# Where a kernel's one-hot tiles begin in SBUF: moving them by 64 bytes, with every instruction left in its place

## The chip, the cores and the metric

The kernel runs on one core of a Trainium2 chip, as one program. The metric is the device time of one execution in microseconds; lower is better. The time before is 1871.04 us, the median of three runs (1870.9 to 1872.39).

## What is computed

The reference is a small decoder of two layers over 256 tokens of 1024 features, in float32. Each layer is a mixer (sparse and block attention in layer 0, latent attention in layer 1) and then a PEER channel mixer, which takes most of the time and is the only part that the change touches:

```python
q = (xc @ w_q).reshape(t, 8, 2, 128)                    # 8 heads, two halves
sc = einsum('thpc,hpnc->thpn', q, sub_keys)             # 128 keys a half
...                                                     # top 16 of each half, top 16 of their sums
g = softmax(top_s)                                      # 16 gates a head: 128 of 16384 experts a token
u = u_tab[expert]
act = gelu(einsum('thkd,td->thk', u, xc))
w = g * act
return einsum('thk,thkd->td', w, v_tab[expert])
```

The kernel does not gather experts. It computes all 16384 activations of every token, multiplies them by a dense matrix of gates (zero for experts that were not chosen), and multiplies the result by the whole `v_tab`.

## The kernel before, in words

**Exact products from split operands.** A float32 product is made of three passes in the format fp32r: both operands are split into a high part and a low rest (`hi`, `lo`), and high by high, high by rest and rest by high are added up in PSUM. Weights arrive by DMA in tiles `raw` of 128x1024, in three buffers. `Weights.split` (L69 on ScalarE, L70 on VectorE) turns each half of such a tile into a 128x512 `hi` and `lo`, five buffers of each.

**The PEER block, once a layer (`peer`).** Its stretches follow each other on TensorE:

1. Queries: 16 products S of `w_q` with the tokens (`rhi`, `rlo`: 8 chunks of 128x256 each, not normalised), and scores of each query (L1052) against the sub-keys. VectorE takes the top 16 (`stage1`).
2. Blocks: the loop `for b in range(NK)` over 128 blocks of 128 experts. A block is 24 matmuls (L823 to L825): a 128x128 piece of a weight tile is loaded as the stationary operand, and the 256 tokens (`hi`, `lo`, normalised) stream through as the moving operand. The result S goes into the block of `A` by `put_act`.
3. Gates, worked in between the blocks as a background job (`gates`, pumped by `bg.pump(PB)` after each half block): for four tokens at a time, one-hots over the first key (`E`, a tile `ohB`, bf16) and one-hots times gate (`G`, a tile `ohA`, fp16) are made by VectorE (L986 to L1001) and, for every second group, partly by ScalarE (L980, L982). Eight matmuls of 128 columns (L1015, into `scp`) then make the dense gates of the four tokens: `E` is the stationary operand and `G` the moving one. There are 64 such groups a layer, and each stands between two of the matmuls of step 2.
4. Output: `wsplit(b)` splits block b of `A` into a high and a low part (L1092, L1093), into tiles with the names `ohA` and `ohB` too. They are the stationary operand of 12 matmuls of 512 columns a block (L1103 to L1105), with the split rows of `v_tab` as the moving operand; the sum over all blocks stays in four PSUM banks `acc`.

**Where tiles lie.** A pool's tiles lie one behind the other in each partition's bytes. A tile without use (`fill...`) only pushes what comes after it. So the start addresses of the tiles, taken modulo 512 bytes (the residue below), are:

| tiles | role on TensorE | residue before | residue after |
|---|---|---|---|
| `hi`, `lo` of the weights, `raw`, `A[0]` | stationary in blocks, moving in the output | 160 | 160 |
| `rhi`, `rlo`, `hi0`.., `lo0`.. (tokens) | moving in queries and blocks | 96 | 96 |
| `ohB`, `ohA` as one-hots `E`, `G` | stationary and moving of the gates | 160 | 96 |
| `ohA`, `ohB` as split activations | stationary in the output | 160 | 160 |
| `act` (queries, and a helper tile of `put_act`) | stationary in the scores | 160 | 96 |
| `A[1]` (blocks 104 to 127) | none | 160 | 96 |

Within these tiles every operand that TensorE reads starts at a multiple of 512 bytes from the tile's start (or, for the split activations after the change, from 64 bytes into it), so one residue holds for all operands of a row. The second token of a pair in `E` and `G` lies 2 bytes further.

Of the kernel before, what the change touches and what calls it, by code (L numbers as in the profile page):

```python
# [9 lines left out]
F32 = mybir.dt.float32  # L10
F32R = mybir.dt.float32r
# [135 lines left out]
def body(tc, I, out):  # L147
    nc = tc.nc
    with ExitStack() as ctx:
# [24 lines left out]
        for k, v in PLAN1:  # L174
            if k == "P" and v[0] == "c":
                add(I["w1"][int(v[1])], 352)
            elif k == "P":
                n = "uq" if v[0] == "q" else "ukv"
# [102 lines left out]
        def tiles8(pool, name, dtype=F32R):  # L281
            return [pool.tile([128, S], dtype, name=f"{name}{c}") for c in range(8)]
# [475 lines left out]
        def peer(layer, gcol, final=False):  # L758
            with ExitStack() as c1:
# [6 lines left out]
                def scr(n):  # L766
                    o = off[0]
                    off[0] += n
                    assert off[0] <= (NA - SCR) * S, off
                    return flat[:, o:o + n]  # L770

                hp = c1.enter_context(tc.tile_pool(name="hp", bufs=1))
                ohp = c1.enter_context(tc.tile_pool(name="ohp", bufs=2))
# [3 lines left out]
                RE, RM = hp.tile([128, S], BF, name="RE"), hp.tile([128, 2, S], F16, name="RM")  # L777
                RA = hp.tile([128, 3, 4 * len(GA)], F32, name="RA")

                hp.tile([128, 112], F32, name="fill0")  # L780
                hi, lo = tiles8(hp, "hi"), tiles8(hp, "lo")
                hp.tile([128, 16], F32, name="fill1")
                rawc = ExitStack()
                rawpool = rawc.enter_context(tc.tile_pool(name="rawt", bufs=1))
                rawpool.tile([128, 112], F32, name="fill2")
                scv = scr(2 * 16 * 128)
                sc = scv.rearrange("p (a b c) -> p a b c", a=2, b=16)
                sk = scr(2048).rearrange("p (j n) -> p j n", j=16)
# [176 lines left out]
                def gates():  # L965
                    def hot(t0, E, G):
                        pr = lambda r: r.rearrange("p (q t) -> p q t", t=2)[:, :, None, :]
                        bc = lambda r: pr(r[:, t0:t0 + 4]).to_broadcast([128, 2, 128, 2])
                        io = lambda n: iotaX[:, None].to_broadcast([128, n, 128, 2])
                        act = t0 // 4 in GA  # L970
                        e = E[:, 1]
                        if act:
                            k = 4 * GA.index(t0 // 4)

                        def pair(i, relu):
                            if act:
                                for j in (i, i + 1):
                                    r = [RA[:, n, k + j:k + j + 1] for n in range(3)]
                                    if relu:
                                        nc.scalar.activation(e[:, j // 2, :, j % 2], e[:, j // 2, :, j % 2], AF.Relu, bias=r[1], scale=r[2])  # L980
                                    else:
                                        nc.scalar.activation(e[:, j // 2, :, j % 2], iota, AF.Square, bias=r[0], scale=-1.0)  # L982

                        pair(0, False)
                        if act:
                            nc.vector.tensor_tensor(E[:, 0], io(2), pr(R1[:, t0 // 4, 0]).to_broadcast([128, 2, 128, 2]),  # L986
                                                    op=OP.is_equal)
                        else:
                            nc.vector.tensor_tensor(E.rearrange("p s q i t -> p (s q) i t"), io(4),
                                                    pr(R1[:, t0 // 4].rearrange("p s t -> p (s t)")).to_broadcast([128, 4, 128, 2]),  # L990
                                                    op=OP.is_equal)
                        yield YA if act else 0.6
                        pair(2, False)
                        nc.vector.tensor_tensor(G[:, 0], E[:, 0], bc(RM[:, 0]), op=OP.mult)
                        yield YA if act else 0.34
                        pair(0, True)
                        nc.vector.tensor_tensor(G[:, 1], E[:, 0], bc(RM[:, 1]), op=OP.mult)
                        yield YA if act else 0.34
                        pair(2, True)
                        if not act:  # L1000
                            nc.vector.tensor_tensor(e, e, bc(RE), op=OP.mult)  # L1001
                        yield YA if act else 0.34

                    def tiles():
                        return [ohp.tile([128, 4, 128], F32, name=n).rearrange("p t i -> p (t i)").bitcast(d).rearrange(
                            "p (s q i t) -> p s q i t", s=2, q=2, t=2) for n, d in (("ohB", BF), ("ohA", F16))]

                    nxt = tiles()
                    yield from hot(0, *nxt)
                    for t0 in range(0, S, 4):  # L1010
                        E, G = nxt
                        p = ps2.tile([128, 512], F32, name="scp").rearrange("p (t i) -> p t i", t=4)
                        for i in range(4):
                            for s in range(2):
                                nc.tensor.matmul(p[:, i], E[:, 1, i // 2, :, i % 2], G[:, s, i // 2, :, i % 2], start=i + s == 0, stop=True,  # L1015
                                                 skip_group_check=True)
                        if t0 + 4 < S:
                            nxt = tiles()
                            yield from hot(t0 + 4, *nxt)
                        for k, (c, e) in enumerate(((0, NA), (NA, NK))):  # L1020
                            n = min(max(done[0], c), e)
                            if n < e:
                                nc.scalar.activation(A[k][:, n - c:, t0:t0 + 4],
                                                     p[:, :, n:e].rearrange("p t i -> p i t"), AF.Copy)
                            if n > c:
                                a = A[k][:, :n - c, t0:t0 + 4]
                                nc.vector.tensor_tensor(a, a, p[:, :, c:n].rearrange("p t i -> p i t"), op=OP.mult)
                        done[1] = t0 + 4
                        yield 0.5

                def block(b):
                    return A[0][:, b] if b < NA else A[1][:, b - NA]
# [28 lines left out]
                for j in range(16):  # L1061
                    p = ps2.tile([128, 512], F32, name="S")[:, :S]
# [17 lines left out]
                for b in range(NK):  # L1080
                    p = ps2.tile([128, 512], F32, name="S")[:, :S]
# [6 lines left out]
                bg.drain()  # L1088

                def wsplit(b):  # L1090
                    t = ohp.tile([128, 4, 128], F32, name="ohA" if b % 2 else "ohB").rearrange("p (s h) e -> p s (h e)", s=2).bitcast(F32R)
                    nc.scalar.activation(t[:, 0], block(b), AF.Copy)  # L1092
                    nc.vector.tensor_tensor(t[:, 1], block(b), t[:, 0].bitcast(F32), op=OP.subtract)  # L1093
                    return t

                ws = [wsplit(0), wsplit(1)]
                put_act(*prev)
                acc = [[ps2.tile([128, 512], F32, name="acc", bufs=4) for _ in range(2)] for _ in range(2)]
# [8 lines left out]
                for b in range(NK - 2):  # L1107
                    a = ws.pop(0)
                    for dh in range(2):
                        w = W.next()  # L1110
                        if dh == 0:
                            ws.append(wsplit(b + 2))
                        for tb in range(2):
                            mm(b, a, w, tb, dh)
# [5 lines left out]

        even_mixer(0)
        peer(0, 16)
        mla_mixer(8)
        peer(1, 24, True)


# [59 lines left out]
```

## Time and profile before

| what | value |
|---|---|
| time, median of three runs | 1871.04 us (1870.9 to 1872.39) |
| the profiled execution: its time, its span | 1871.02 us, 1869.2 us |
| TensorE busy with matmuls | 1845.6 us, 99% of the span |
| VectorE, ScalarE, GpSimd busy | 1431.8, 1245.3, 15.0 us |
| mean granted clock of TensorE | 0.998 of full speed |
| matmuls L823, L824, L825 on `hi`, `lo` (blocks) | 2048 each |
| matmuls L1015 (gates) | 1024 |
| matmuls L1103 to L1105 (output) | 3072 |

The span is the time from the first to the last instruction; 1.8 us of the profiled time lie outside it. A matmul's busy time in the profile runs from its start to the arrival of its last result, so those of neighbours overlap, and the rate of a stream of matmuls is read from the distance of their starts.

### The profile page before, as it was taken

What the parts mean: (1) busy time and instruction counts of PE and PEld (TensorE: products, weight loads), DVE (VectorE), ACT (ScalarE), POOL (GpSimd) and SP (SyncE); (2) the same over time, 40 slices, a digit from 0 to 9 for tenths busy, and PEclk for the clock granted to TensorE, in tenths of its full rate; (3) what the DMA queues carried; (4) which work ended last, traced back from release to release, by engine and by line L of the source; (5) the groups of instructions that cost most, each with busy time, mean ns of one, the idle gap of its engine ahead of it and who ended that gap; (6) DMA issues with size and microseconds to landing.
All of it is one profiled execution on the core that took longest, in us unless ns stands there. A gap on an engine that the chain in (4) does not pass through costs nothing.

```text
span 1869.2 us, 35589 instructions
## 1 busy us (share of the span) xinstructions
PE 1845.6 (99%) x12568; PEld 1668.6 (89%) x12568; DVE 1431.8 (77%) x3586; ACT 1245.3 (67%) x3060; POOL 15.0 (1%) x34
## 2 busy tenths in 40 slices
PE   9999999999999999999999999999999999999998
PEld 7779999999999888888888899999999988888886
DVE  7968998878897666666677699987888976666665
ACT  5656567888886555555577665688888765555554
POOL 0000000000000000000000000000000000000000
PEclk9999999999999999999999999999999999999999
DMA  6434555555555556565553345655545555555554
GB/s 197 130 112 147 177 188 180 170 168 161 167 161 180 192 193 195 193 195 193 183 170 124 125 148 186 194 170 164 166 161 169 167 183 192 193 193 196 195 192 148
DMA packets 90178, 323.33 MB, mean 173 GB/s; under 512 B 10512, under 2 KB 10896, under 8 KB 89744
## 3 DMA queue, kind: packets, MB, share of 16 engines
q1 hardware_dynamic: 88416, 318.18, 52.9%
q8 instruction: 99, 1.62, 0.4%
q0 software_dynamic: 288, 2.10, 0.3%
q10 hardware_dynamic: 1296, 0.78, 0.1%
q14 instruction: 79, 0.65, 0.1%
HBM read 319.97 MB, written 1.05 MB: 172 GB/s over the span
## 4 chain that ended last, share of the span: by engine, by line
PE 93%; DVE 4%; ACT 1%; issue 1%; DMA 0%; POOL 0%; DVEq 0%; POOLq 0%; ACTq 0%
PE S L823 14%; PE S L825 14%; PE S L824 14%; PE acc L1103 12%; PE acc L1104 12%; PE acc L1105 12%; PE scp L1015 3%; PE pj L301 2%; PE pj L303 2%; PE pj L302 2%; DVE lo L70 1%; PE bk L375 1%; PE scp L1052 1%; PE pj L439 1%; PE pj L440 1%
## 5 line engine op out<-in xcount | busy, mean ns | idle before, releaser
L69 ACT ACTIVATE hi<-raw 128x512 fp32r<-128x512 f32 (+2 forms) x1214 | 755.3, 628 | 562.7 <-DVE lo L70 190.4
L70 DVE TENSOR_TENSOR lo<-raw,hi 128x512 fp32r<-128x512 f32 (+2 forms) x1214 | 825.1, 684 | 361.7 <-ACT hi L69 354.0
L823 PE MATMUL S<-hi,hi 128*128 128x256 f32 x2048 | 584.9, 286 | 0.6 <-ACT A L1044 0.6
L825 PE MATMUL S<-hi,lo 128*128 128x256 f32 x2048 | 575.4, 281 | 0.5
L824 PE MATMUL S<-lo,hi 128*128 128x256 f32 x2048 | 574.4, 281 | 0.0
L825 PEld LDWEIGHTS S<-hi,lo 128*128 128x128 f32 x2048 | 387.2, 189 | 1.7 <-DVE lo L70 1.7
L824 PEld LDWEIGHTS S<-lo,hi 128*128 128x128 f32 x2048 | 388.6, 190 | 0.0
L823 PEld LDWEIGHTS S<-hi,hi 128*128 128x128 f32 x2048 | 385.1, 188 | 1.1 <-ACT A L1044 1.0
L1104 PE MATMUL acc<-lo,ohB 128*128 128x512 f32 x512 | 199.2, 389 | 0.0
L1104 PE MATMUL acc<-lo,ohA 128*128 128x512 f32 x512 | 199.2, 389 | 0.0
L1105 PE MATMUL acc<-hi,ohA 128*128 128x512 f32 x512 | 198.8, 389 | 0.0
L1105 PE MATMUL acc<-hi,ohB 128*128 128x512 f32 x512 | 198.2, 389 | 0.0
L1103 PE MATMUL acc<-hi,ohB 128*128 128x512 f32 x512 | 158.3, 389 | 0.0
L1103 PE MATMUL acc<-hi,ohA 128*128 128x512 f32 x512 | 158.0, 389 | 0.0
L980 ACT ACTIVATE ohB<-ohB,RA 128x128 bf16<-128x128 bf16 x256 | 117.4, 527 | 0.0
L1105 PEld LDWEIGHTS acc<-hi,ohB 128*128 128x128 f32 x512 | 96.2, 188 | 20.0
L1104 PEld LDWEIGHTS acc<-lo,ohA 128*128 128x128 f32 x512 | 96.2, 188 | 19.9
L1103 PEld LDWEIGHTS acc<-hi,ohB 128*128 128x128 f32 x512 | 96.1, 188 | 19.9
L1103 PEld LDWEIGHTS acc<-hi,ohA 128*128 128x128 f32 x512 | 96.1, 188 | 20.0
L1105 PEld LDWEIGHTS acc<-hi,ohA 128*128 128x128 f32 x512 | 96.0, 188 | 19.9
L1104 PEld LDWEIGHTS acc<-lo,ohB 128*128 128x128 f32 x512 | 96.1, 188 | 19.8
L982 ACT ACTIVATE ohB<-iota,RA 128x128 bf16<-128x128 f32 x256 | 84.2, 436 | 0.0
(261 smaller groups left out, 2409.3 us busy)
## 6 DMA issues: line engine op xcount, KB each, us to landing
raw<-in_pu SPq DMA_DIRECT2D x256, 512.0 KB, 3.6
raw<-in_pv SPq DMA_DIRECT2D x256, 512.0 KB, 4.3
raw<-in_pq SPq DMA_DIRECT2D x32, 512.0 KB, 3.6
raw<-in_w SPq DMA_DIRECT2D x20, 512.0 KB, 3.8
raw<-in_uq SPq DMA_DIRECT2D x9, 512.0 KB, 4.3
raw<-in_w SPq DMA_DIRECT2D x12, 352.0 KB, 3.0
raw<-in_w0o SPq DMA_DIRECT2D x8, 512.0 KB, 3.5
raw<-in_w1o SPq DMA_DIRECT2D x8, 512.0 KB, 3.6
```

Of the source, the lines that this page charges most:

```text
L69: self.nc.scalar.activation(hi[:, :w], src, AF.Copy)
L70: self.nc.vector.tensor_tensor(lo[:, :w], src, hi[:, :w].bitcast(F32), op=OP.subtract)
L301: nc.tensor.matmul(ps[tb], hi[c][:, t], a, start=st, stop=False)
L823: nc.tensor.matmul(p, a, hi[c], start=first and i == 0, stop=False)
L824: nc.tensor.matmul(p, a, lo[c], start=False, stop=False)
L825: nc.tensor.matmul(p, b, hi[c], start=False, stop=last and i == 3)
L980: nc.scalar.activation(e[:, j // 2, :, j % 2], e[:, j // 2, :, j % 2], AF.Relu, bias=r[1], scale=r[2])
L982: nc.scalar.activation(e[:, j // 2, :, j % 2], iota, AF.Square, bias=r[0], scale=-1.0)
L1015: nc.tensor.matmul(p[:, i], E[:, 1, i // 2, :, i % 2], G[:, s, i // 2, :, i % 2], start=i + s == 0, stop=True, skip_group_check=True)
L1103: nc.tensor.matmul(o, a[:, 0, t], w[0], start=b == 0, stop=False)
L1104: nc.tensor.matmul(o, a[:, 0, t], w[1], start=False, stop=False)
L1105: nc.tensor.matmul(o, a[:, 1, t], w[0], start=False, stop=b == NK - 1)
```

## The change

The change takes out two filling tiles and enlarges the one-hot tiles from 512 to 640 float32 words. The one-hots use the first 512 words of a tile. The split activations use the words from 16 to 528, which are 64 bytes further on. Without `fill1` the pool `ohp` begins at the tokens' residue; its tiles (2 x 1024 and 4 x 2560 bytes) are a multiple of 512 bytes together, so the pool behind it keeps the tokens' residue without `fill2`.

```diff
                 hp.tile([128, 112], F32, name="fill0")
                 hi, lo = tiles8(hp, "hi"), tiles8(hp, "lo")
-                hp.tile([128, 16], F32, name="fill1")
                 rawc = ExitStack()
                 rawpool = rawc.enter_context(tc.tile_pool(name="rawt", bufs=1))
-                rawpool.tile([128, 112], F32, name="fill2")
...
                     def tiles():
-                        return [ohp.tile([128, 4, 128], F32, name=n).rearrange("p t i -> p (t i)").bitcast(d).rearrange(
+                        return [ohp.tile([128, 640], F32, name=n)[:, :512].bitcast(d).rearrange(
                             "p (s q i t) -> p s q i t", s=2, q=2, t=2) for n, d in (("ohB", BF), ("ohA", F16))]
...
                 def wsplit(b):
-                    t = ohp.tile([128, 4, 128], F32, name="ohA" if b % 2 else "ohB").rearrange("p (s h) e -> p s (h e)", s=2).bitcast(F32R)
+                    t = ohp.tile([128, 640], F32, name="ohA" if b % 2 else "ohB")[:, 16:528].rearrange("p (s e) -> p s e", s=2).bitcast(F32R)
```

No instruction is added, taken out or moved: on each engine and on each DMA queue the instructions of the two programs stand in the same order, with the same shapes and the same engines waited for. They differ in addresses alone (and in line numbers, which are smaller by one behind the edit).

## Rows read from the trace of the kernel before

**Rows 1.** The page's busy times, and its chain that ended last.

```profile
PE 1845.6 (99%) x12568; PEld 1668.6 (89%) x12568; DVE 1431.8 (77%) x3586; ACT 1245.3 (67%) x3060; POOL 15.0 (1%) x34
PE 93%; DVE 4%; ACT 1%; issue 1%; DMA 0%; POOL 0%; DVEq 0%; POOLq 0%; ACTq 0%
```

**Rows 2.** Gate stretches: start:end, length, busy us (count) of PE, PEld, DVE, ACT, POOL.

```profile
306.00:585.00 279.00, 279.00 (x2601) 276.17 (x2599) 236.83 (x557) 231.77 (x709) 0.00 (x0) 1.00 0.52 165
...
1230.00:1509.00 279.00, 279.00 (x2600) 276.17 (x2599) 236.72 (x557) 231.78 (x708) 0.00 (x0) 1.00 0.52 165
```

**Rows 3.** Timeline of TensorE from 216 us: first and last of 104 matmuls (start, us).

```profile
215.76 0.28 PE L825 MATMUL S<-hi,lo 128*128 128x256 f32 x1
...
227.89 0.28 PE L823 MATMUL S<-hi,hi 128*128 128x256 f32 x1
```

**Rows 4.** The same from 276 us: first and last of 109 matmuls.

```profile
275.74 0.28 PE L823 MATMUL S<-hi,hi 128*128 128x256 f32 x1
...
287.98 0.28 PE L823 MATMUL S<-hi,hi 128*128 128x256 f32 x1
```

**Rows 5.** L824 from 216 to 246 us, then from 276 to 288 us (busy, mean ns).

```profile
L824 PE MATMUL S<-lo,hi 128*128 128x256 f32 x85 | 23.8, 281 | 0.0
...
L824 PE MATMUL S<-lo,hi 128*128 128x256 f32 x36 | 9.9, 276 | 0.0
```

**Rows 6.** TensorE's groups from 308 to 584 us, then one from 1230 to 1508 us.

```profile
L824 PE MATMUL S<-lo,hi 128*128 128x256 f32 x690 | 193.9, 281 | 0.0
L825 PE MATMUL S<-hi,lo 128*128 128x256 f32 x689 | 193.8, 281 | 0.0
L1015 PE MATMUL scp<-ohA,ohB 128*128 128x128 f16 x498 | 39.9, 220 | 0.0
...
L824 PE MATMUL S<-lo,hi 128*128 128x256 f32 x695 | 195.3, 281 | 0.0
```

**Rows 7.** Timeline around two groups of gates of layer 0; then around one of layer 1.

```profile
323.37 0.63 PE L1015 MATMUL scp<-ohA,ohB 128*128 128x128 f16 x8
...
324.48 0.28 PE L825 MATMUL S<-hi,lo 128*128 128x256 f32 x1
...
325.16 0.28 PE L825 MATMUL S<-hi,lo 128*128 128x256 f32 x1
325.28 0.63 PE L1015 MATMUL scp<-ohA,ohB 128*128 128x128 f16 x8
...
325.92 0.28 PE L824 MATMUL S<-lo,hi 128*128 128x256 f32 x1
...
326.74 0.28 PE L825 MATMUL S<-hi,lo 128*128 128x256 f32 x1
...
1247.25 0.63 PE L1015 MATMUL scp<-ohA,ohB 128*128 128x128 f16 x8
...
1248.37 0.28 PE L825 MATMUL S<-hi,lo 128*128 128x256 f32 x1
...
1248.71 0.28 PE L825 MATMUL S<-hi,lo 128*128 128x256 f32 x1
```

**Rows 8.** Timeline behind two groups of scores in layer 1's query stretch.

```profile
1068.00 0.28 PE L824 MATMUL S<-rlo,hi 128*128 128x256 f32 x1
...
1069.70 0.28 PE L824 MATMUL S<-rlo,hi 128*128 128x256 f32 x1
1069.93 0.60 PE L1052 MATMUL scp<-A,act 128*128 128x128 f32 x4
...
1070.56 0.28 PE L824 MATMUL S<-rlo,hi 128*128 128x256 f32 x1
...
1071.27 0.28 PE L824 MATMUL S<-rlo,hi 128*128 128x256 f32 x1
```

**Rows 9.** Groups of the output stretch from 600 to 900 us.

```profile
L1104 PE MATMUL acc<-lo,ohA 128*128 128x512 f32 x220 | 85.6, 389 | 0.0
L1105 PE MATMUL acc<-hi,ohA 128*128 128x512 f32 x220 | 85.6, 389 | 0.0
```

## The prediction

> **What bounds the kernel now.** I read the page first. TensorE's matmuls cover 99% of the span, and 93% of the chain that ended last is TensorE's [rows 1]. So what counts is how densely TensorE's matmuls follow each other; the other engines count only where TensorE waits for them. The change touches the block stretch with its gates (one a layer), so I asked for the busy time there. In both stretches TensorE is covered without a hole at the full granted clock, while VectorE works 237 of 279 us and ScalarE 232 [rows 2]. TensorE has to be made faster there, or nothing is.
>
> The timeline shows at what rate it works, and here is something that a share of busy time hides. The same matmul, L823 to L825, runs in two rhythms. From 215.76 to 227.89 us there are 103 distances of starts in 12.13 us: 117.8 ns each [rows 3]. From 275.74 to 287.98 us there are 108 in 12.24 us: 113.3 ns [rows 4]. Shapes, operands and residues are the same in both. The groups show it too: a matmul lasts 281 ns in the slow rhythm and 276 in the fast one [rows 5]. In both gate stretches the means of L824 and L825 are 281 [rows 6], so at least nine in ten of those matmuls are in the slow rhythm.
>
> A rhythm lasts until something interrupts the stream, and the first matmuls behind the interruption set the next one. In the gate stretches the interruptions are the 64 groups of gates a layer. The group at 323.37 us is followed by the fast rhythm (324.48 to 325.16 us: 6 distances in 0.68 us, 113 ns), the group at 325.28 us by the slow one (325.92 to 326.74 us: 7 in 0.82 us, 117 ns) [rows 7]. The same group of layer 1, at 1247.25 us, is followed by the fast one again (3 in 0.34 us) [rows 7]. So the choice is not noise: it repeats at the same place of the program. Behind other interruptions both rhythms occur: between two groups of scores the stream is fast (1068.00 to 1069.70 us: 15 distances, 113 ns), behind the second of these groups slow (1070.56 to 1071.27 us: 6, 118 ns) [rows 8].
>
> **The change part by part.**
>
> *Instructions.* None is added, removed or moved, and no wait changes. The filling tiles cost no instruction; the larger tiles cost memory alone. This is 0 us.
>
> *Work of VectorE and ScalarE on one-hots, `act` and `A[1]`, now 64 bytes lower.* No row has one of these instructions at both residues. Their cover is VectorE's 42 us and ScalarE's 47 us of idle time in each gate stretch [rows 2]: all their work there would have to grow by 18 to 20% before TensorE waited. Likewise faster writes would give nothing. I take 0.
>
> *Output stretch.* The split activations keep residue 160, but half of the new tiles begin 512 bytes off their old place modulo 1024. The stationary operand takes such steps already: L1104 reads the high part, L1105 the low part 1024 bytes behind it, each at two places 512 bytes apart, and both last 389 ns [rows 9]. I take 0. If the steady rate were lost, each of the 3072 matmuls is two streams of 256 columns long, and the difference of the two rhythms, 4.5 ns a stream, would make 3072 x 9 ns = 28 us. I give that no more than 3 in 100 and leave it out of the range.
>
> *The gates' own matmuls.* Stationary `E` and moving `G` lay at 160 and both lie at 96 now, so inside a group of eight nothing changes in relation to each other: 0. For bounds, a step as large as that between the rhythms, 4.5 ns, on each of the 1024 of them is 4.6 us either way.
>
> *The hand-overs.* This is where the change can act. The first weights behind a group (residue 160) are loaded while the last `G` streams: both at 160 before, 160 against 96 now. The latter is the relation that weights and tokens have all through the blocks. And the first `E` is loaded while tokens stream: 160 against 96 before, both at 96 now. If weight loads and moving reads disturb each other by address, the hand-overs shift by some nanoseconds, and a hand-over decides between 113.3 and 117.8 ns for all that follows up to the next group. From 308 to 584 us there are 690 of L824, so some 2,070 matmuls of L823 to L825, and 2,085 in the other stretch [rows 6]: 4,155 together. At nine tenths in the slow rhythm, 3,740 x 4.5 ns = 16.8 us is all that can be won. Falling either way by halves, as behind other interruptions, would win 0.4 x 4,155 x 4.5 ns = 7.5 us. Losing the last tenth costs 0.1 x 4,155 x 4.5 ns = 1.9 us.
>
> Which end? The present order of residues sends nearly every hand-over the slow way, which is an extreme; new relations can hardly make it more so. I take the middle of the two upper ends, 12 us.
>
> The Trainium skill speaks against any effect. Its page "TensorE: Matmul & The Clock Gate" (section "Step-by-step: what each phase is for") has two independent read ports, one for the moving operand and one for weight loads, so that loading the next weights takes nothing from the running matmul. Its section "Back-to-back issue gap" gives columns / 2.4 + 2.5 ns, an estimate of 109.2 ns for 256 columns. By the first rule addresses could not matter and the sum would be 0; the trace has neither rhythm at the second's figure, so something does hold these pairs of load and matmul back. No run here shows yet whether it is an address.
>
> **Sum.** 0 + 0 + 0 + 0 - 12 us, from the profiled execution's 1871.02 us (span 1869.2 and 1.8 outside), which is the median of the runs to 0.02 us: 1859 us.
>
> **The rivals.**
>
> *A. The hand-overs turn (my forecast).* For it: the choice is made within nanoseconds, is the same at the same place in both layers, and the change alters just what TensorE reads at that moment. Own range 1853 to 1865 us: 16.8 us and something from the gates' matmuls at one end, 7.5 us less 1.5 for other stretches at the other.
>
> *B. Nothing turns.* TensorE's two reads may not meet by address, or the shift leaves the hand-overs on the slow side, as they are now. For it: a rhythm changes without any change of address [rows 3, 4], so timing alone decides, and no row shows a residue at work. Against it: a choice this one-sided [rows 6] has a fixed cause, and the operands at the hand-over are the nearest one. Time 1871.0, by 1.9 us for the last tenth of the slow rhythm, and as much the other way: 1869 to 1873 us. By the skill's rule of two ports this is the outcome.
>
> *C. The gates' loads collide (slower).* `E` is now loaded against tokens, and `G` streams against loads, at other relations than before. If each gate matmul loses the step between the rhythms, and the rest of the fast rhythm goes too, 1024 x 4.5 ns + 1.9 us = 6.5 us: 1877.5 us. It decides from 3.7 us on, which is 3.6 ns on each gate matmul or 29 ns on each of the 128 hand-overs. Against it: the pair `E`, `G` keeps its relation.
>
> **How the numbers follow.** A 0.46, B 0.37, C 0.17. What a measurement can tell from no change is about 0.2%, 3.7 us; the three cases lie on its three sides, so these are the chances of faster, same and slower. The predicted time is A's, 1859 us. The range has to reach into all three cases: from A's lower end, 1853, to 1877. That leaves out about half of C's case and the tails of A, less than 2 in 10.
>
> **What would show it.** If A holds, L824 and L825 in the gate stretches drop from 281 towards 276 ns, distances of starts between groups are 113 ns, and both gate stretches shrink by 4 to 8 us each, while the output stretch, VectorE's and ScalarE's busy times keep their size. If B holds, the means stay at 281 and the two groups of [rows 7] keep their rhythms. If C holds, L1015 lasts longer than 220 ns or its groups longer than 0.63 us. I am wrong if the stretch of queries or the output moves more than the gate stretches do, or if the same rhythms come out with another time.

## The result, and the profile of the changed kernel

The changed kernel takes 1860.51 us (median of four runs, 1858.68 to 1863.23), the kernel before 1871.55 us on the same chip (1870.9 to 1872.39): a ratio of 0.994 with a 95% interval of 0.9928 to 0.9953. That is 11.0 us less. The forecast was 1859 us. Ratios here are taken over undisturbed runs.

The page shows less time on TensorE and the same bound. Busy times first, then the chain that ended last:

```profile
PE 1834.3 (99%) x12568; PEld 1657.3 (89%) x12568; DVE 1431.0 (77%) x3586; ACT 1244.5 (67%) x3060; POOL 14.5 (1%) x34
PE 92%; DVE 5%; ACT 1%; issue 1%; DMA 0%; POOL 0%; DVEq 0%; POOLq 0%; ACTq 0%
```

Against [rows 1] the count of instructions is the same. TensorE has 11.3 us less to do and remains covered to 99%; VectorE and ScalarE keep their work to 0.8 us. So neither a wait nor another engine's work has changed: the same matmuls have become denser.

Where? The view of one line's instructions gives the first and the last start of the gates' matmul in each layer (count, min/median/max ns, starts in us). In the kernel before:

```profile
L1015 PE MATMUL scp<-ohA,ohB x512: 217/218/233, 307.5 to 585.0; 128*128 128x128 f16 x171
...
L1015 PE MATMUL scp<-ohA,ohB x512: 217/218/233, 1231.4 to 1508.8; 128*128 128x128 f16 x171
```

In the changed kernel (the line has moved up by one):

```profile
L1014 PE MATMUL scp<-ohA,ohB x512: 218/218/233, 310.4 to 581.4; 128*128 128x128 f16 x171
...
L1014 PE MATMUL scp<-ohA,ohB x512: 218/218/233, 1227.6 to 1498.6; 128*128 128x128 f16 x171
```

Each gate stretch has shrunk by 6.4 us, together 12.8 us: by the trace's nanoseconds, which the view rounds, from 277.49 to 271.08 us in either layer. What lies between the two stretches takes 646.4 us before and 646.1 us after, and what lies behind them 360.3 and 360.2. The first group of gates starts 2.9 us later. So the spans differ by 6.4 + 6.4 + 0.3 + 0.1 - 2.9 = 10.3 us (1869.2 to 1858.9). The late start isn't the change's doing as far as the runs can tell: 2.5 of the 2.9 us are there at the first query matmul of layer 0 (136.8 and 139.3 us), and in eight kernels below that differ from the changed one only in addresses of one-hots, the first group starts anywhere from 306.8 to 310.8 us.

The busy time in both stretches, as in [rows 2] but for ends that have moved:

```profile
306.00:585.00 279.00, 279.00 (x2653) 276.41 (x2653) 242.27 (x574) 237.75 (x726) 0.00 (x0) 1.00 0.53 169
...
1230.00:1505.00 275.00, 275.00 (x2599) 271.99 (x2598) 238.44 (x564) 232.71 (x710) 0.00 (x0) 1.00 0.53 169
```

The same 279 us hold 2,653 matmuls where they held 2,601, at the same full granted clock. TensorE is still without a hole, and the other engines keep 36 us or more of idle time in 279. The groups from 308 to 584 us, to set beside [rows 6] (count, busy us, mean ns):

```profile
L823 PE MATMUL S<-lo,hi 128*128 128x256 f32 x706 | 196.0, 278 | 0.0
L824 PE MATMUL S<-hi,lo 128*128 128x256 f32 x706 | 195.9, 278 | 0.0
...
L1014 PE MATMUL scp<-ohA,ohB 128*128 128x128 f16 x512 | 40.9, 220 | 0.0
```

The gates' matmul has kept its 220 ns. The mean of the block matmuls has dropped from 281 to 278 ns, which is more than half of the way to the 276 ns of a stream that is wholly in the fast rhythm [rows 5]. Now count the distances from the start of a block matmul to the next start in the gate stretch of layer 0, in the trace's nanoseconds. Before, 133 were fast (up to 115 ns) and 1,818 slow (116 to 121 ns); now 1,534 are fast and 464 slow. The other distances, about 200 ns directly behind each group and some of 122 to 125 ns at the groups, are in neither count.

The timeline shows one hand-over: the group that stood at 325.28 us before and sent the stream into the slow rhythm [rows 7] (start, duration).

```profile
327.68 0.63 PE L1014 MATMUL scp<-ohA,ohB 128*128 128x128 f16 x8
328.12 0.36 PE L822 MATMUL S<-hi,hi 128*128 128x256 f32 x1
...
328.56 0.28 PE L822 MATMUL S<-hi,hi 128*128 128x256 f32 x1
...
331.96 0.28 PE L822 MATMUL S<-hi,hi 128*128 128x256 f32 x1
...
346.16 0.46 PE L1014 MATMUL scp<-ohA,ohB 128*128 128x128 f16 x5
...
347.93 0.35 PE L1014 MATMUL scp<-ohA,ohB 128*128 128x128 f16 x3
...
348.52 0.28 PE L822 MATMUL S<-hi,hi 128*128 128x256 f32 x1
...
352.05 0.28 PE L822 MATMUL S<-hi,hi 128*128 128x256 f32 x1
```

From 328.56 to 331.96 us there are 30 distances in 3.40 us: 113.3 ns. The group itself costs what it did, 0.44 us from its first matmul to the first block matmul. The last four rows show where the remaining slow matmuls come from. A group that is split in two by block matmuls (5 of its matmuls at 346.16, 3 at 347.93 us) is followed by 30 distances in 3.53 us, 117.7 ns, and the stream stays slow for several groups. So before the change nearly every hand-over ended slow, from either rhythm: 58 of the 66 in a layer (two of the 64 groups are split), among them 8 of the 9 that found a fast stream. After it a hand-over mostly keeps the rhythm that it finds: 51 keep a fast one and 11 a slow one, 2 turn it slow and 2 turn it fast.

The places of the turns are fixed by the program. The two that turn slow in the changed kernel stand at the two split groups. Turns to fast have a mark of their own. Eight groups a layer stand between two of the three passes of one product, all others behind the third pass. In the eleven kernels of this document that show the two rhythms, every turn from slow to fast is at one of these eight, at a part of a split group, or at the group right behind one of those. Why that is so no run shows.

Output: L1103 and L1104 from 600 to 900 us, 389 ns as in [rows 9].

```profile
L1103 PE MATMUL acc<-lo,ohA 128*128 128x512 f32 x222 | 86.4, 389 | 0.0
L1104 PE MATMUL acc<-hi,ohA 128*128 128x512 f32 x222 | 86.4, 389 | 0.0
```

### The profile page after: what moved, and what is told of

It is laid out like the page before. It is cut to its first block, busy times and chain, and to the rows that moved or that the text cites. A ratio compares the mean times of both kernels' runs of the same rounds, so it can differ in the third digit from the quotient of the medians.

```text
span 1858.9 us, 35589 instructions
## 1 busy us (share of the span) xinstructions
PE 1834.3 (99%) x12568; PEld 1657.3 (89%) x12568; DVE 1431.0 (77%) x3586; ACT 1244.5 (67%) x3060; POOL 14.5 (1%) x34
## 4 chain that ended last, share of the span: by engine, by line
PE 92%; DVE 5%; ACT 1%; issue 1%; DMA 0%; POOL 0%; DVEq 0%; POOLq 0%; ACTq 0%
PE S L822 14%; PE S L824 13%; PE S L823 13%; PE acc L1102 12%; PE acc L1104 12%; PE acc L1103 12%; PE scp L1014 3%; PE pj L301 2%; PE pj L303 2%; PE pj L302 2%; DVE lo L70 1%; PE bk L375 1%; PE pj L439 1%; PE scp L1051 1%; PE pj L440 1%
## 5 line engine op out<-in xcount | busy, mean ns | idle before, releaser
L824 PE MATMUL S<-hi,lo 128*128 128x256 f32 x2048 | 569.8, 278 | 0.4 <-DVE lo L70 0.2
L823 PE MATMUL S<-lo,hi 128*128 128x256 f32 x2048 | 568.8, 278 | 0.0
L824 PEld LDWEIGHTS S<-hi,lo 128*128 128x128 f32 x2048 | 385.3, 188 | 1.7 <-DVE lo L70 1.4
L823 PEld LDWEIGHTS S<-lo,hi 128*128 128x128 f32 x2048 | 385.3, 188 | 0.0
L1103 PE MATMUL acc<-lo,ohB 128*128 128x512 f32 x512 | 199.2, 389 | 0.0
L1103 PE MATMUL acc<-lo,ohA 128*128 128x512 f32 x512 | 199.2, 389 | 0.0
L1104 PE MATMUL acc<-hi,ohA 128*128 128x512 f32 x512 | 198.8, 389 | 0.0
L1104 PE MATMUL acc<-hi,ohB 128*128 128x512 f32 x512 | 198.2, 389 | 0.0
L1103 PEld LDWEIGHTS acc<-lo,ohA 128*128 128x128 f32 x512 | 96.1, 188 | 20.0
L1103 PEld LDWEIGHTS acc<-lo,ohB 128*128 128x128 f32 x512 | 96.1, 188 | 19.9
L1104 PEld LDWEIGHTS acc<-hi,ohA 128*128 128x128 f32 x512 | 96.1, 188 | 19.9
L1104 PEld LDWEIGHTS acc<-hi,ohB 128*128 128x128 f32 x512 | 96.0, 188 | 19.9
```

Source lines behind the costliest of these rows:

```text
L823: nc.tensor.matmul(p, a, lo[c], start=False, stop=False)
L824: nc.tensor.matmul(p, b, hi[c], start=False, stop=last and i == 3)
L1103: nc.tensor.matmul(o, a[:, 0, t], w[1], start=False, stop=False)
L1104: nc.tensor.matmul(o, a[:, 1, t], w[0], start=False, stop=b == NK - 1)
```

## The experiments

All are the changed kernel with other addresses. No instruction differs between them in kind or order; e5, without a filling tile, has line numbers smaller by one. In the edits, `o` is the first word of the slice of a one-hot tile, so a residue is 96 + 4 x `o`. The time of an experiment is the median of 4 to 10 executions beside the kernel before, which took 1871.97 to 1872.41 us in these sessions. "Gates" is the first to the last start of the gates' matmul by the trace's nanoseconds, layer 0 and layer 1.

| kernel | residue of `E`, `G` | tokens | us | ratio (95%) | gates, us |
|---|---|---|---|---|---|
| before | 160, 160 | 96 | 1871.55 | | 277.5, 277.5 |
| changed | 96, 96 | 96 | 1860.51 | 0.994 (0.9928 to 0.9953) | 271.1, 271.1 |
| e1 | 160, 160 | 96 | 1873.26 | 1.0002 (0.9993 to 1.0012) | 277.5, 277.5 |
| e2 | 96, 160 | 96 | 1872.72 | 1.0001 (0.9992 to 1.0011) | 277.4, 277.4 |
| e3 | 160, 96 | 96 | 1873.09 | 1.0002 (0.9992 to 1.0011) | 277.2, 277.2 |
| e4 (split activations 96) | 96, 96 | 96 | 1868.28 | 0.998 (0.9969 to 0.999) | 271.1, 271.1 |
| e5 | 160, 160 | 160 | 1888.46 | 1.0087 (1.007 to 1.0104) | 282.0, 282.0 |
| e6 (512 bytes on) | 96, 96 | 96 | 1859.53 | 0.9927 (0.991 to 0.9944) | 271.1, 271.1 |
| e7 | 352, 352 | 96 | 1859.51 | 0.993 (0.9913 to 0.9946) | 271.1, 271.1 |
| e8 | 128, 128 | 96 | 1860.32 | 0.9937 (0.9921 to 0.9954) | 271.1, 271.1 |
| e9 | 416, 416 | 416 | 1888.68 | 1.0089 (1.0073 to 1.0106) | 282.0, 282.0 |
| e10 | 32, 32 | 32 | 1884.37 | 1.0066 (1.0049 to 1.0082) | 280.9, 280.9 |
| e11 | 96, 352 | 96 | 1859.14 | 0.9935 (0.9919 to 0.9952) | 271.1, 271.1 |
| e12 | 32, 96 | 96 | 1858.0 | 0.9926 (0.9909 to 0.9942) | 270.8, 270.8 |

**e1: only the one-hots back.** `act`, `A[1]` and the larger tiles stay as changed.

```diff
-ohp.tile([128, 640], F32, name=n)[:, :512]      # E and G: o = 0
+ohp.tile([128, 640], F32, name=n)[:, 16:528]    # E and G: o = 16
```

> The changed kernel with the one-hots read 64 bytes further into their tiles, so that both E and G lie at residue 160 again; everything else (act, A[1], the raw tokens, the split activations) stays where the change put it. Theory (the residue of the one-hots decides what rhythm the block matmuls take behind a group of gates): the gate stretches go back to the slow rhythm, mean of L823 and L824 281 ns, time 1871 us, within 2. Rival (some other move of the change did it: act, A[1], the raw tokens): time 1860 us, mean 278 ns.

The whole gain is gone. The group of L823 from 320 to 575 us stands at the 281 ns of [rows 6]:

```profile
L823 PE MATMUL S<-lo,hi 128*128 128x256 f32 x637 | 179.0, 281 | 0.0
```

In the gate stretch of layer 0, 133 distances are fast and 1,818 slow, exactly as in the kernel before. So the one-hots' residue alone makes the difference; `act`, `A[1]` and the size of the tiles do nothing that can be measured.

**e2 and e3: one operand of the gates back.** In e2 the moving operand `G` returns to 160, in e3 the stationary `E`.

```diff
-(("ohB", BF, 0), ("ohA", F16, 0))     # changed: E, G
+(("ohB", BF, 0), ("ohA", F16, 16))    # e2
+(("ohB", BF, 16), ("ohA", F16, 0))    # e3
```

> Only the stationary one-hots E at 96, the moving G back at 160. If the load of the first E beside the last tokens decides: 1860 us, rhythm as in the changed kernel. If the load of the first block weights (160) beside the last G decides: 1871 us, rhythm as before. If the relation of E to G inside a group decides, neither: the distances inside a group (57 ns) change too.

> The mirror: only the moving G at 96, the stationary E back at 160. If the load of the first block weights beside the last G decides (the relation the weights have with tokens all through a block; my first choice, 6 in 10): 1860 us. If the load of the first E beside the tokens decides: 1871 us.

Each alone brings the slow rhythm back: 258 fast distances are left in e2, 249 in e3. In e2's timeline, behind a group:

```profile
327.22 0.64 PE L1014 MATMUL scp<-ohA,ohB 128*128 128x128 f16 x8
...
328.10 0.28 PE L822 MATMUL S<-hi,hi 128*128 128x256 f32 x1
...
330.93 0.28 PE L822 MATMUL S<-hi,hi 128*128 128x256 f32 x1
```

24 distances in 2.83 us, 117.9 ns. Besides, a group of eight takes 447 ns (e3: 444; medians) to the first block matmul, where it took 441 before and 443 in the changed kernel. By e2 alone the load behind the last `G` would decide, by e3 alone that of the first `E`; so neither of the two hand-overs that I had named decides alone, and my first choice, by which e3 would have taken 1860 us, missed. These two runs leave open whether 160 is harmful in itself or only `E` and `G` at different places; e12 takes that up.

**e4: the split activations moved along with the one-hots.**

```diff
-t = ohp.tile([128, 640], F32, name="ohA" if b % 2 else "ohB")[:, 16:528]...
+t = ohp.tile([128, 640], F32, name="ohA" if b % 2 else "ohB")[:, 0:512]...
```

> The changed kernel, but the split activations begin at their tiles' start, residue 96, while the split rows of v_tab that stream beside them stay at 160. If residues matter in the output stretch: its 3072 matmuls leave 226.7 ns; with a step of 4.5 ns on each the time would be 1874 us, with 9 ns 1888 us. If they matter only at hand-overs: 1860 us, output distances unchanged.

The gate stretches keep the gain, yet the time is 7.8 us longer than the changed kernel's. Most of that is the output. Its groups, 600 to 900 us:

```profile
L1103 PE MATMUL acc<-lo,ohB 128*128 128x512 f32 x220 | 86.5, 393 | 0.0
L1104 PE MATMUL acc<-hi,ohB 128*128 128x512 f32 x220 | 86.0, 391 | 0.0
L1102 PE MATMUL acc<-hi,ohB 128*128 128x512 f32 x220 | 68.0, 390 | 0.0
```

They last 390 to 393 ns instead of 389, and the starts are 228.9 ns apart instead of 226.7: 3072 x 2.2 ns = 6.8 us. The effect is there, but none of the times that I had expected (1860, 1874, 1888 us): the step is half of the 4.5 ns that I had taken for the smaller one. The part of the change that looks idle, the split activations' 64 bytes, is what kept this.

**e5: everything at the weights' residue.** The filling tile ahead of the weights goes, so that the tokens lie at the weights' residue too.

```diff
-hp.tile([128, 112], F32, name="fill0")
-...[:, 16:528].rearrange("p (s e) -> p s e", s=2)    # split activations
+...[:, 0:512].rearrange("p (s e) -> p s e", s=2)
```

> The changed kernel without fill0 and with the split activations at their tiles' start: tokens, one-hots, split activations and weights all at residue 160. In the output stretch a load and a stream at one residue hold the faster of the rates seen (226.7 ns for 512 columns; 228.9 with 64 bytes between them). If equal residues are good for the blocks too, every block matmul runs at 113.3 ns: some 2,200 slow ones are left in the changed kernel, 9.8 us, so 1851 us. If a load that lasts as long as its stream of 256 columns wants the 64 bytes, blocks are slower than 117.8 ns all through: with another 4.5 ns on 6,900 of them, 1895 us or more.

This is slower than before, by 0.87%, and neither of the times that I had expected (1851, or 1895 and more). First and last of 103 block matmuls from the blocks ahead of the first gates:

```profile
215.72 0.28 PE L821 MATMUL S<-hi,hi 128*128 128x256 f32 x1
...
227.96 0.28 PE L821 MATMUL S<-hi,hi 128*128 128x256 f32 x1
```

12.24 us by 102 distances are 120.0 ns, a third rhythm, and in the gate stretches not one distance is fast. Here nothing is left to a hand-over: with tokens and weights at one residue each matmul pays, 2.2 ns more than in the slow rhythm.

**e6, e7: how far an address counts.**

```diff
-(("ohB", BF, 0), ("ohA", F16, 0))
+(("ohB", BF, 128), ("ohA", F16, 128))   # e6: 512 bytes on
+(("ohB", BF, 64), ("ohA", F16, 64))     # e7: residue 352
```

> The changed kernel with the one-hots 512 bytes further into their tiles, so the residue modulo 512 stays 96. If the residue modulo 512 is all that counts: the same 1860 us, gate stretches of 271.1 us with the same fast and slow matmuls. If a longer period counts (1024 bytes): anything else, up to 1872 us.

> One-hots E and G both at 352: equal to each other, but neither at the tokens' residue 96 nor at the weights' 160. If it only matters that they are off the weights' residue: 1860 us. If they have to stand at the tokens' residue: 1871 us.

Both are the changed kernel again (271.1 us a stretch). For e6 that is as the residue modulo 512 has it. e7 was meant to be a new place, and by e9 below it isn't one: 352 and 96 are 256 bytes apart.

**e8: a residue that is neither the weights' nor the tokens'.**

```diff
+(("ohB", BF, 8), ("ohA", F16, 8))       # residue 128
```

> One-hots both at 128, halfway between the tokens' 96 and the weights' 160. If addresses count in steps of 64 bytes or more (96 and 128 then fall into one or two such steps): exactly the 1860 us of the changed kernel or exactly the 1871 us of before. If in finer steps: a third pattern of rhythms behind the groups, between 1855 and 1872 us.

The gain is the same: the tokens' residue is not needed, it is enough to be off 160. The way to it differs, though, so 32 bytes do count. 1,630 distances are fast and 315 slow, and a group takes 446 ns instead of 443: behind nearly every group four distances of 117 to 123 ns follow the first, and then the stream is fast.

**e9 and e10: the tokens at two other distances from the weights**, the one-hots with them. In e9 they are 256 bytes from the weights, in e10 128. The split activations stay at 160.

```diff
-hp.tile([128, 112], F32, name="fill0")  # one-hots o = 0, split activations o = 16
+hp.tile([128, 64], F32, name="fill0")   # e9: split activations o = 64
+hp.tile([128, 96], F32, name="fill0")   # e10: split activations o = 32
```

> The changed kernel with another fill0, so that tokens, act and one-hots lie at 416, half of 512 away from the weights' 160 (split activations stay at 160). So far: tokens and weights at one residue gave 120.0 ns for every block matmul, 64 bytes apart gave either 117.8 or 113.3. If two reads meet only when they start close together, half a period apart has 113.3 ns alone: 9.8 us less than the changed kernel, 1851 us. If the order after a hand-over is what counts, not the distance: both rhythms still occur, 1855 to 1875 us.

> The same with tokens, act and one-hots at 32, 128 bytes below the weights. If a larger distance is better: between 1851 and 1860 us with fewer slow matmuls. If 64 bytes was the best distance: 1860 to 1888 us.

e9 repeats e5 (its group of L823 from 320 to 590 us):

```profile
L823 PE MATMUL S<-lo,hi 128*128 128x256 f32 x664 | 188.0, 283 | 0.0
```

Its distances are 120.0 ns and its gate stretches 282.0 us, as in e5. Both outcomes that I had expected (1851, or 1855 to 1875 us) missed. So 256 bytes away is the same place, and the residue that counts here is that modulo 256, not 512. e10 is a mixture of 115 to 122 ns, mostly 119 to 121: of the distances tried, only that of 64 bytes gives the two rhythms of 117.8 and 113.3 ns.

**e11 and e12: `E` and `G` apart, but neither at the weights' residue.**

```diff
+(("ohB", BF, 0), ("ohA", F16, 64))      # e11: E 96, G 352
+(("ohB", BF, 112), ("ohA", F16, 0))     # e12: E 544 = 32, G 96
```

> The changed kernel with E at 96 and G at 352: unequal, but neither at the weights' 160. In the two runs with one of them at 160 the gate stretches were as long as before, and E and G were unequal there too. If standing at the weights' residue is what hurts: 1860 us, gate stretches near 271 us. If their being unequal hurts: 1872 us, near 277 us.

> The changed kernel with E at 32 and G at 96: 64 bytes apart, as in the two runs with one operand back at 160, but neither at the weights' 160 (tokens at 416 ran as tokens at 160 do, so addresses count modulo 256, and 352 stood for 96 in the two runs that used it). If an operand at the weights' residue is what sends the stream into the slow rhythm: gate stretches near 271 us, 1860 us. If E and G being unequal does it: near 277 us, 1872 us, with groups of 444 to 446 ns instead of 441 as in those two runs.

e11 is 96 and 96 again modulo 256 and shows no more than that. e12 decides: `G` lies 64 bytes above `E`, as in e2, and a group takes 446 ns, about as there (447), but the stream behind it turns fast. Its timeline:

```profile
326.78 0.64 PE L1014 MATMUL scp<-ohA,ohB 128*128 128x128 f16 x8
...
327.66 0.28 PE L822 MATMUL S<-hi,hi 128*128 128x256 f32 x1
...
328.69 0.28 PE L822 MATMUL S<-hi,hi 128*128 128x256 f32 x1
...
330.74 0.28 PE L822 MATMUL S<-hi,hi 128*128 128x256 f32 x1
```

From 327.66 to 328.69 us 9 distances take 1.03 us, 114.4 ns with slow ones among the first; from 328.69 to 330.74 us 18 take 2.05 us, 113.9 ns. 1,687 distances are fast and 259 slow. So unequal residues cost a few ns a group and don't hold the stream slow; in e2 it is left to `G` at 160. For `E` (e3) the mirror of e12 wasn't run. And 160 is two things at once, the weights' residue and 64 bytes above the tokens'; no run parts the two, so that it is the weights' residue that counts for the one-hots is not shown. e12 has the best median, 1858.0 us, but its interval overlaps that of the changed kernel: no better version is claimed.

## Why the prediction was right

*The bound* held. TensorE's rate was all that counted: 12.8 us won in its gate stretches and 0.4 us elsewhere are, less the 2.9 us of a later start, the span's 10.3.

*Hand-overs turn (my forecast A)* held. The rhythms are the same two, 117.8 and 113.3 ns; the share of fast distances rose from 133 of 1,951 to 1,534 of 1,998, and e1 shows that the one-hots' residue does it. 1,354 distances fewer in the slow rhythm, at 4.5 ns, are 6.1 of the 6.4 us of a stretch.

*The size* was right by a choice, not by a mechanism. I took 12 us as the middle of "falls either way" (7.5) and "all fast" (16.8), and the gate stretches gave 12.8. That these lie close together is luck. The true picture is neither: a hand-over mostly keeps the rhythm that it finds, which the prediction had nowhere, and the turns are at fixed places of the program, so that the length of the stretch repeats to 0.1 us from e6 to e7 and e11.

*The reason within it* fell in one point. I had the first weights behind a group, loaded while the last `G` streams, as the first of two places, and gave it the greater weight in what I expected of e3. By e2 and e3 neither hand-over suffices alone: `G` alone at 160 leaves the stream slow, and `E` alone at 160 leaves it slow too. Nor was it the tokens' residue that helped (e8, e12).

*Zeros.* Instructions, VectorE's and ScalarE's work, and the inside of a group (441 and 443 ns to the first block matmul, 0.3 us in all) were 0 or next to it, as said. The output was 0 too (389 ns), because the split activations kept their residue; the half of their new tiles that is off by 512 bytes costs nothing, as e6 shows it for the one-hots. I had priced a lost rate there at 28 us; where the rate was lost, by a move of 64 bytes (e4), it cost 6.8 us.

*Rival B* (nothing turns) is what e1 to e3 measure, and its argument that a rhythm changes without a change of address was true and beside the point: address sets how a hand-over falls, and the rhythm that it finds does the rest. The Trainium skill's page "TensorE: Matmul & The Clock Gate", section "Step-by-step: what each phase is for", has loads of weights and reads of the moving operand on independent ports. If that were all, as the prediction read it, addresses could not matter; here the addresses of one-hots alone make 11 us of 1871, and tokens at the weights' residue slow every block matmul from 117.8 or 113.3 to 120.0 ns. The 109.2 ns that the prediction took from the Trainium skill, the same page's section "Back-to-back issue gap", is by that section the gap of a single matmul by itself; of a stream of loads and matmuls it says that both set the spacing. So rhythms above 109.2 ns were no sign yet that something holds the pairs back. *Rival C* (gates' loads collide) fell: 220 ns and 0.63 us are unchanged.

Still open: what in the chip compares these addresses; why a hand-over keeps its rhythm, and why it turns at split groups and behind those between two passes; whether one-hots at 160 hurt because of the weights or because of the tokens; and tokens 64 bytes above the weights, which wasn't tried.

## What to carry to other kernels

When TensorE is covered without a hole and still the same matmul lasts 276 ns here and 281 there, read the distances of starts, and look for what interrupts the stream where the rhythm changes. Then try start addresses: here an unused tile or a slice added no instruction. There is no one best distance to carry over. In the blocks (256 columns), the moving operand 64 bytes below the stationary one modulo 256 was the best of the distances tried, with the small interposed matmuls off the weights' residue. In the output (512 columns) equal residues were better than the stationary operand 64 bytes below, 226.7 ns against 228.9. So check every use of a tile that is moved: the split activations, in the same tiles, wanted their old place (e4).

## What was not expected of the hardware

An address modulo 256 bytes sets the pace of a stream of 256-column matmuls: tokens at the weights' residue, 120.0 ns for all; 64 bytes below, 117.8 or 113.3; 128 away, mostly 119 to 121. And a stream remembers: in the changed kernel, eight gate matmuls of 0.44 us mostly leave it in the rhythm that it had, for tens of block matmuls on either side (62 of 66 hand-overs in a layer), and the gate stretches of five kernels (changed, e4, e6, e7, e11) are the same to 0.1 us.
